# Softmax left unnormalised until after the value product, and the low part of q laid out on all 128 rows

## The chip, the cores and the metric

The kernel runs on one core of one Trainium2 chip. The metric is the time of one execution on the device in microseconds; three runs give a median. One further execution was taken by the hardware profiler, and every row below is from it.

## The reference

One decoder layer for 1024 tokens of width 1024, all in float32. The change lies in the attention, of which this is the part that matters (8 heads of 64):

```python
h = x @ w_in[i]                              # columns [q | k | v | u | z]
q = _partial_rope(q, positions); k = _partial_rope(k, positions)
scores = einsum(q, k) * (1.0 / math.sqrt(dh))        # three dilations, (window, dilation):
scores = where(mask, scores, NEG_INF)                # (128, 1), (512, 4), (2048, 16), causal
e = jnp.exp(scores - m)
den = jnp.sum(e, axis=-1, keepdims=True)
out = einsum(e / den, vb); lse = m + jnp.log(den)
attn = sum over dilations of softmax(lse) * out      # merged by the log-sum-exp weights
mix = jnp.concatenate([attn, gm], axis=-1) @ w_o[i]  # gm: a gated MLP beside the attention
x = _layernorm(ALPHA * x + mix, ln1_g[i], ln1_b[i])
```

Behind it come a gated feed-forward layer with a causal convolution over 2816 columns, a gate with a per-layer embedding, and two more layer norms.

## The kernel before

**Numbers in two parts.** TensorE multiplies in a reduced float32 (F32R). Each operand is therefore split into a high part, a rounded copy, and a low part, the rest. A full product is three matmuls into one PSUM bank (mm3, lines 132 to 134): high by high, high by low, low by high.

**Attention.** The merged dilations are one softmax over 1024 keys with an additive mask (0, log 2 or log 3 where one, two or three dilations see a key). Queries go in four row blocks I of 256 tokens (two parts of 128), and a unit is one row block and one head: 32 units, in order of I, then of head. Head h sits in pair p = h // 2; its 64 dimensions are partitions 0 to 63 for even heads and 64 to 127 for odd ones.

- K is kept as KE and KO. For even heads KE has K's high part in rows 0 to 63 and its low part in rows 64 to 127; KO is the mirror image for odd heads.
- q_post (line 452) transposes a block of q and writes QE and QO, which hold q's high part twice, and QL, which holds the low part of an even head in rows 0 to 63 and of the odd head of the same pair in rows 64 to 127. It is called from a list of slots (posts, line 881). Its ACT copies are issued at once, its DVE operations (rest) one slot later.
- unit_S (line 661) makes scores in chunks of up to 512 keys: L688 multiplies q's high part twice by K's high and low part (128 rows), L689 multiplies q's low part by K's high part alone (64 rows). DVE adds the mask, negates and takes the running minimum (L698).
- unit_exp (line 702) takes the exponential on ACT with the row sum in `den`, and unit_norm (line 707), one slot after it, takes the reciprocal (a power on POOL, L710) and multiplies both parts of the probabilities by it on POOL (L712).
- unit_T (line 714) transposes four 128 x 128 blocks of the probabilities on TensorE (L719); ACT and DVE split them.
- unit_PV (line 545) multiplies by V (L557). V's high and low part lie side by side, so rows 0 to 63 and 64 to 127 of the bank O each hold one part of the output, and unit_out (line 560) adds the two: ACT copies one half to `ot`, DVE adds (L570) into the mixture's page.

**What sets the order.** The schedule is manual: every engine runs its instructions in program order, and semaphores are added for the data. `attention` (line 743) goes through slots. In a slot it issues the scores of a unit up to three ahead, the DVE operations put off from the slot before (`later`), the exponentials and normalisations that are due, one unit_T, the unit_PV of three slots before, then a number of steps (pump) of a queue that fills TensorE: first the projections of q (q_dense, whose rotary embedding, rope, runs six operations on POOL), then, from unit 17 on, the output projections of finished row blocks (wo_up). `sides` advance beside it: the layer norm of finished blocks and the splits of the output weights on POOL (L537). The last row block's projection, wo_up(3), follows attention.

**Buffers.** Most tiles of attention are pages of 4 KB per partition, 24 in all under one tag: the parts of x not yet used, V's second half, q, the scores, the split probabilities. The banks S and O have two buffers each, and the transposes use three.

Of the kernel before, what the change touches and what calls it, by code (L numbers as in the profile page):

```python
# [51 lines left out]
def hybrid_layer(ctx, tc, x, xT, pT, pos, w_in, ln_z_g, ln_z_b, w_sT, b_sT, w_o,  # L52
# [98 lines left out]
    POOL.memset(neghalf, -0.5)  # L151
    negone = consts.tile([128, 2], F32, name="negone")
    POOL.memset(negone, -1.0)
# [295 lines left out]

    QE, QO, QL = {}, {}, {}  # L450

    def q_post(j, t):
        tok = q_toks[j]
        if t == 0:
            QE[j] = page([128, 4, 256], F32R, "qe")
            QO[j] = page([128, 4, 256], F32R, "qo")
            QL[j] = page([128, 4, 256], F32R, "ql")
        qe, qo, ql = QE[j], QO[j], QL[j]
        kt = tok_T(tok, t, "T")
        ts = slice(t * 128, (t + 1) * 128)  # L460
        copy(ACT, qe[0:64, :, ts], kt[0:64])
        copy(ACT, qo[64:128, :, ts], kt[64:128])
        copy(ACT, qo[0:64, :, ts], kt[64:128])

        def rest():
            copy(DVE, qe[64:128, :, ts], kt[0:64])
            DVE.tensor_tensor(ql[0:64, :, ts], kt[0:64], qe[0:64, :, ts].bitcast(F32), OP.subtract)
            DVE.tensor_tensor(ql[64:128, :, ts], kt[64:128], qo[64:128, :, ts].bitcast(F32), OP.subtract)
        return rest
# [70 lines left out]

    unit_state = {}

    mixes = {}

    def unit_PV(I, h, m, pt):
        st = unit_state[I, h]
        if m == 0:
            st["o"] = ps1("O")
        o = st["o"]
        for kb in (2 * m, 2 * m + 1):  # L550
            full = kb <= 2 * I
# [4 lines left out]
            for hl in range(2):  # L556
                PE.matmul(osl, v, pt[:, hl, src:src + wd], start=kb == 0 and hl == 0,  # L557
                          stop=kb == 2 * I + 1 and hl == 1)

    def unit_out(I, h):  # L560
# [5 lines left out]
        r, r2 = (slice(64, 128), slice(0, 64)) if odd else (slice(0, 64), slice(64, 128))  # L566
        ot = small.tile([128, 256], F32, name="ot", bufs=1)
        copy(ACT, ot[r], o[r2, 0:256])
        mix = mixes[I][r, p, :]
        later.append(lambda: DVE.tensor_tensor(mix, o[r, 0:256], ot[r], OP.add))  # L570

# [89 lines left out]
    def unit_S(I, h, chunk):  # L661
# [6 lines left out]
        K = KO if odd else KE  # L668
        r = slice(64, 128) if odd else slice(0, 64)
        q_lo = QL[I][r, p, ts]  # L670
        if part == 0 and c0 == 0:
            st["den"] = small.tile([128, 2], F32, name="den", bufs=5)
            st["nmx"] = small.tile([128, 4], F32, name="nmx", bufs=5)
# [14 lines left out]
        PE.matmul(o, q_hi, K[:, p, c0:c0 + w_], start=True, stop=False)  # L688
        PE.matmul(o, q_lo, K[r, p, c0:c0 + w_], start=False, stop=True)  # L689
        m0 = S - n + c0  # L690
# [11 lines left out]
    def unit_exp(I, h, part):  # L702
        st = unit_state[I, h]
        ACT.activation(st[part], st[part], AF.Exp, bias=st["m", part], scale=-1.0,
                       accum_out=st["den"][:, part:part + 1])

    def unit_norm(I, h):
        st = unit_state[I, h]
        rd = small.tile([128, 2], F32, name="rd", bufs=4)
        POOL.tensor_tensor(rd, st["den"], negone, OP.pow)  # L710
        for part in range(2):
            POOL.tensor_scalar(st[part], st[part], rd[:, part:part + 1], 1.0, op0=OP.mult, op1=OP.mult)  # L712

# [15 lines left out]
    due = []  # L729
# [13 lines left out]
    def attention(plan):  # L743
# [12 lines left out]
        for n in range(-3, len(units)):  # L756
# [8 lines left out]
            for m in range(banks):  # L765
# [8 lines left out]
                for v, ch in news[:take]:  # L774
                    if ch[3]:
                        due.append((slot + 1, "e", lambda v=v, p=ch[0]: unit_exp(*units[v], p)))
                        if ch[0] == 1:
                            due.append((slot + 2, "n", lambda v=v: unit_norm(*units[v])))
                news = news[take:]
# [633 lines left out]
```

## Time and profile before

| | |
|---|---|
| median of 3 runs | 1254.71 us (1254.49 to 1255.15) |
| the profiled execution | 1254.94 us |
| its span, first to last instruction | 1253.2 us |
| TensorE matmul busy | 1229.5 us, 98% |
| VectorE (DVE) busy | 795.9 us, 64% |
| ScalarE (ACT) busy | 539.4 us, 43% |
| GpSimd (POOL) busy | 546.3 us, 44% |
| mean granted clock of TensorE | 0.995 |

PE is TensorE's matmuls, PEld its weight loads. Times in the rows are us from the span's start unless marked ns. Matmuls overlap in the pipeline: the time of one runs from its start to its modelled end, so what a matmul costs in a stream is the distance to the next start. A bracket at the end of a timeline row is the time that the engine was idle before it and what released it; "issue" means that nothing the profile shows did. An entry x4 in a timeline merges four instructions.

### The profile page before, as it was taken

What the parts mean: (1) busy time and instruction counts of PE and PEld (TensorE: products, weight loads), DVE (VectorE), ACT (ScalarE), POOL (GpSimd) and SP (SyncE); (2) the same over time, 40 slices, a digit from 0 to 9 for tenths busy, and PEclk for the clock granted to TensorE, in tenths of its full rate; (3) what the DMA queues carried; (4) which work ended last, traced back from release to release, by engine and by line L of the source; (5) the groups of instructions that cost most, each with busy time, mean ns of one, the idle gap of its engine ahead of it and who ended that gap; (6) DMA issues with size and microseconds to landing.
All of it is one profiled execution on the core that took longest, in us unless ns stands there. A gap on an engine that the chain in (4) does not pass through costs nothing.

```text
span 1253.2 us, 15740 instructions
## 1 busy us (share of the span) xinstructions
PE 1229.5 (98%) x5804; PEld 1001.2 (80%) x5804; DVE 795.9 (64%) x1194; ACT 539.4 (43%) x921; POOL 546.3 (44%) x467
## 2 busy tenths in 40 slices
PE   9999999999999997999999999999999999999997
PEld 6888788877777777888888888888878888888886
DVE  4544422346877789566565566555667985797776
ACT  5322122367855663544434444444444354541221
POOL 2510000255727769576677776677610000022444
PEclk9999999999999998999999999999999999999998
DMA  7215511200200221221333321333479544640001
GB/s 272 68 51 183 185 35 35 68 18 1 85 35 17 85 101 68 69 85 55 114 126 126 127 64 63 126 127 126 133 261 313 205 129 126 228 159 17 35 34 51
DMA packets 61005, 131.70 MB, mean 105 GB/s; under 512 B 5376, under 2 KB 23168, under 8 KB 60928
## 3 DMA queue, kind: packets, MB, share of 16 engines
q1 hardware_dynamic: 58480, 122.17, 28.3%
q10 hardware_dynamic: 2448, 8.52, 2.0%
q8 instruction: 46, 0.75, 0.2%
q14 instruction: 31, 0.25, 0.1%
HBM read 97.90 MB, written 32.77 MB: 104 GB/s over the span
## 4 chain that ended last, share of the span: by engine, by line
PE 59%; DVE 2%; POOL 1%; issue 0%; ACT 0%; POOLq 0%; ACTq 0%
PE P L133 9%; PE P L134 9%; PE P L132 9%; PE D L134 7%; PE D L132 7%; PE D L133 7%; PE B L134 3%; PE B L132 3%; PE B L133 3%; PE B L860 1%; PE x2p L1266 0%; DVE th L1294 0%; DVE xop L868 0%; DVE wraw L951 0%; POOL rs L585 0%
## 5 line engine op out<-in xcount | busy, mean ns | idle before, releaser
L132 PE MATMUL P<-xop,wop 128*128 128x512 f32 (+1 forms) x360 | 138.9, 386 | 0.0
L134 PE MATMUL P<-xop,wop 128*128 128x512 f32 (+1 forms) x360 | 138.4, 384 | 0.0
L133 PE MATMUL P<-xop,wop 128*128 128x512 f32 (+1 forms) x360 | 138.4, 384 | 0.0
L168 POOL TENSOR_SCALAR rs<-mv 128x1 f32<-128x1 f32 x24 | 12.7, 529 | 265.3 <-DVE mv L166 265.3
L117 POOL TENSOR_TENSOR wop<-raw,wop 128x512 fp32r<-128x512 f32 x64 | 100.6, 1583 | 43.8 <-ACT wop L111 43.7
L117 POOL TENSOR_TENSOR wop<-s,wop 128x512 fp32r<-128x512 f32 x44 | 68.7, 1572 | 72.5 <-ACT wop L111 72.5
L111 ACT ACTIVATE aop<-raw 128x512 fp32r<-128x512 f32 x77 | 48.2, 626 | 91.7 <-DMA raw<-hid_d 56.8
L429 POOL TENSOR_TENSOR rt<-tok,cos_t 128x128 f32<-128x128 f32 x8 | 4.7, 589 | 177.8 <-ACT tok L488 166.7
L132 PEld LDWEIGHTS P<-xop,wop 128*128 128x128 f32 x360 | 67.6, 188 | 13.5 <-ACT ct L111 0.2
L134 PEld LDWEIGHTS P<-xop,wop 128*128 128x128 f32 x360 | 67.6, 188 | 13.4
L133 PEld LDWEIGHTS P<-xop,wop 128*128 128x128 f32 x360 | 67.6, 188 | 13.3
L132 PE MATMUL D<-xop,wop 128*128 128x512 f32 (+1 forms) x192 | 74.7, 389 | 0.0
L134 PE MATMUL D<-xop,wop 128*128 128x512 f32 (+1 forms) x192 | 73.8, 385 | 0.0
L133 PE MATMUL D<-xop,wop 128*128 128x512 f32 (+1 forms) x192 | 73.8, 384 | 0.0
L1014 POOL TENSOR_TENSOR ht<-ht,ct 128x1024 f32<-128x1024 f32 x22 | 65.9, 2994 | 15.2 <-ACT ht L1011 15.2
L133 PE MATMUL P<-bop,aop 128*128 128x512 f32 x176 | 68.7, 390 | 0.6 <-DVE bop L117 0.6
L117 DVE TENSOR_TENSOR aop<-raw,aop 128x512 fp32r<-128x512 f32 x77 | 54.5, 707 | 22.6 <-ACT aop L111 22.6
L132 PE MATMUL P<-bop,aop 128*128 128x512 f32 x176 | 68.6, 390 | 0.0
L134 PE MATMUL P<-bop,aop 128*128 128x512 f32 x176 | 68.5, 389 | 0.0
L111 ACT ACTIVATE wop<-raw 128x512 fp32r<-128x512 f32 x66 | 40.1, 631 | 63.0 <-DMA raw<-in_w_b_dram 35.5
L117 POOL TENSOR_TENSOR wop<-wraw,wop 128x512 fp32r<-128x512 f32 x44 | 57.0, 1303 | 7.4 <-ACT wop L111 5.1
L698 DVE CUSTOM_DVE_ANT_0 sp<-S,mask 128x512 f32<-128x512 f32 (+2 forms) x64 | 37.0, 588 | 35.7 <-PE S L689 31.7
(316 smaller groups left out, 3528.4 us busy)
## 6 DMA issues: line engine op xcount, KB each, us to landing
raw<-hid_d SPq DMA_DIRECT2D x35, 512.0 KB, 3.8
hid_d<-ct SPq DMA_DIRECT2D x22, 512.0 KB, 5.8
wd<-in_w_down_dram SPq DMA_DIRECT2D x44, 256.0 KB, 5.7
raw<-in_w_in_dram SPq DMA_DIRECT2D x18, 512.0 KB, 3.9
hid_d<-ht SPq DMA_DIRECT2D x33, 256.0 KB, 4.8
raw<-in_w_a_dram SPq DMA_DIRECT2D x11, 512.0 KB, 4.1
raw<-in_w_b_dram SPq DMA_DIRECT2D x11, 512.0 KB, 6.2
wraw<-in_w_a_dram SPq DMA_DIRECT2D x11, 512.0 KB, 6.0
```

Of the source, the lines that this page charges most:

```text
L111: ACT.activation(dst, src, AF.Copy)
L117: lo_eng.tensor_tensor(lo, src, hi.bitcast(F32), OP.subtract)
L132: PE.matmul(ps, sh, mh, start=first, stop=False, skip_group_check=chain)
L133: PE.matmul(ps, sh, ml, start=False, stop=False, skip_group_check=chain)
L134: PE.matmul(ps, sl, mh, start=False, stop=last, skip_group_check=chain)
L168: POOL.tensor_scalar(rs, mv[:, 1:2], eps, None, op0=OP.add)
L429: POOL.tensor_tensor(r[:, 0], x1, cb, OP.mult)
L698: DVE.tensor_tensor_reduce(dst, o, mask[:, m0:m0 + w_], op0=OP.add, op1=OP.min, accum_out=acc, scale=-1.0, scalar=prev)
L860: PE.transpose(ps[:, k * 128:(k + 1) * 128], src[:, k * 128:(k + 1) * 128], ident)
L1014: POOL.tensor_tensor(tt[g, e], tt[g, e], ctile[g, 1, e], OP.mult)
```

## The change

Three things are done. unit_norm goes: the probabilities stay as the exponential leaves them. The sums of both heads of a pair now stand in one tile, POOL takes the four reciprocals at once when the odd head's exponential is issued, and after the even head's last value product POOL spreads them to 64 columns for each head (`rb`); before the odd head's first value product TensorE transposes these two 128 x 128 blocks into the unused half of the odd head's bank O. unit_out then copies one half of the output into the mixture's page on ACT, adds the other on DVE, and for odd heads multiplies the pair's page by the transposed reciprocals on DVE. Last, QL becomes QLE and QLO, in which the low part of each head stands in both halves of the partitions (POOL copies it), so that L689 works on 128 rows and adds the product of the two low parts.

```diff
-    negone = consts.tile([128, 2], F32, name="negone")
+    negone = consts.tile([128, 4], F32, name="negone")
...
-            QL[j] = page([128, 4, 256], F32R, "ql")
+            QLE[j] = page([128, 4, 256], F32R, "qle")
+            QLO[j] = page([128, 4, 256], F32R, "qlo")
...
         def rest():
             copy(DVE, qe[64:128, :, ts], kt[0:64])
-            DVE.tensor_tensor(ql[0:64, :, ts], kt[0:64], qe[0:64, :, ts].bitcast(F32), OP.subtract)
-            DVE.tensor_tensor(ql[64:128, :, ts], kt[64:128], qo[64:128, :, ts].bitcast(F32), OP.subtract)
+            DVE.tensor_tensor(qle[0:64, :, ts], kt[0:64], qe[0:64, :, ts].bitcast(F32), OP.subtract)
+            DVE.tensor_tensor(qlo[64:128, :, ts], kt[64:128], qo[64:128, :, ts].bitcast(F32), OP.subtract)
+            copy(POOL, qle[64:128, :, ts], qle[0:64, :, ts].bitcast(F32))
+            copy(POOL, qlo[0:64, :, ts], qlo[64:128, :, ts].bitcast(F32))
...
         o = st["o"]
+        if m == 0 and h % 2:
+            rb = rbs.pop((I, h // 2))
+            for part in range(2):
+                PE.transpose(o[:, 256 + part * 128:384 + part * 128], rb[:, part, :], ident)
         for kb in (2 * m, 2 * m + 1):
...
+        if m == I and h % 2 == 0:
+            rb = rbs[I, h // 2] = small.tile([128, 2, 128], F32, name="rb", bufs=1)
+            copy(POOL, rb.rearrange("p a (b c) -> p a b c", c=64),
+                 rds.pop((I, h // 2))[:, :, :, None].to_broadcast([128, 2, 2, 64]))
...
-        ot = small.tile([128, 256], F32, name="ot", bufs=1)
-        copy(ACT, ot[r], o[r2, 0:256])
         mix = mixes[I][r, p, :]
-        later.append(lambda: DVE.tensor_tensor(mix, o[r, 0:256], ot[r], OP.add))
+        copy(ACT, mix, o[r2, 0:256])
+        later.append(lambda: DVE.tensor_tensor(mix, o[r, 0:256], mix, OP.add))
+        if odd:
+            both = mixes[I][:, p, :]
+            later.append(lambda: DVE.tensor_tensor(both, both, o[:, 256:512], OP.mult))
...
-        r = slice(64, 128) if odd else slice(0, 64)
-        q_lo = QL[I][r, p, ts]
+        q_lo = (QLO if odd else QLE)[I][:, p, ts]
...
-            st["den"] = small.tile([128, 2], F32, name="den", bufs=5)
+            if not odd:
+                dens[I, p] = small.tile([128, 2, 2], F32, name="den", bufs=4)
+            st["den"] = dens[I, p]
...
-        PE.matmul(o, q_lo, K[r, p, c0:c0 + w_], start=False, stop=True)
+        PE.matmul(o, q_lo, K[:, p, c0:c0 + w_], start=False, stop=True)
...
-                       accum_out=st["den"][:, part:part + 1])
-
-    def unit_norm(I, h):
-        st = unit_state[I, h]
-        rd = small.tile([128, 2], F32, name="rd", bufs=4)
-        POOL.tensor_tensor(rd, st["den"], negone, OP.pow)
-        for part in range(2):
-            POOL.tensor_scalar(st[part], st[part], rd[:, part:part + 1], 1.0, op0=OP.mult, op1=OP.mult)
+                       accum_out=st["den"][:, part, h % 2:h % 2 + 1])
+        if part == 1 and h % 2:
+            rd = rds[I, h // 2] = small.tile([128, 2, 2], F32, name="rd", bufs=5)
+            POOL.tensor_tensor(rd.rearrange("p a b -> p (a b)"),
+                               dens.pop((I, h // 2)).rearrange("p a b -> p (a b)"), negone, OP.pow)
...
-                        if ch[0] == 1:
-                            due.append((slot + 2, "n", lambda v=v: unit_norm(*units[v])))
```

## Rows read from the trace of the kernel before

**Rows 1.** The page, part 1: engine, busy us, share, instructions.
```profile
PE 1229.5 (98%) x5804; PEld 1001.2 (80%) x5804; DVE 795.9 (64%) x1194; ACT 539.4 (43%) x921; POOL 546.3 (44%) x467
```

**Rows 2.** Busy us (count) of PE, PEld, DVE, ACT, POOL; granted clock, DMA share, GB/s.
```profile
330.00:452.00 122.00, 121.75 (x665) 89.36 (x664) 93.83 (x225) 77.86 (x148) 72.24 (x81) 1.00 0.16 57
452.00:505.00 53.00, 44.14 (x290) 39.93 (x289) 49.23 (x63) 23.67 (x46) 48.33 (x38) 0.94 0.27 100
```

**Rows 3.** Timeline of TensorE late in attention: start us, duration us, line.
```profile
428.83 0.39 PE L134 MATMUL D<-wouh,mixl 128*128 128x512 f32 x1
429.06 0.40 PE L688 MATMUL S<-KO,qo 128*128 128x512 f32 x1
429.39 0.50 PE L689 MATMUL S<-KO,ql 64*128 64x512 f32 x1
429.82 0.66 PE L719 MATMUL B<-ident,sp 128*128 128x128 f32 x4
430.23 0.65 PE L557 MATMUL O<-pt,VP 128*128 128x256 f32 x4
```

**Rows 4.** Timeline of TensorE's weight loads, the same slot.
```profile
429.38 0.18 PEld L689 LDWEIGHTS S<-KO,ql 64*128 64x128 f32 x1 [0.36 <-issue]
```

**Rows 5.** Timeline of TensorE early in attention.
```profile
262.24 0.38 PE L689 MATMUL S<-KE,ql 64*128 64x256 f32 x1 [0.33 <-DVE ql L467]
...
264.02 0.22 PE L688 MATMUL S<-KO,qo 128*128 128x128 f32 x1
264.17 0.32 PE L689 MATMUL S<-KO,ql 64*128 64x128 f32 x1
264.42 0.39 PE L688 MATMUL S<-KO,qo 128*128 128x256 f32 x1
264.74 0.38 PE L689 MATMUL S<-KO,ql 64*128 64x256 f32 x1
265.05 0.50 PE L132 MATMUL O<-wih,xh 128*128 128x512 f32 x1
```

**Rows 6.** Tile S: duration ns min/median/max, first and last start, forms.
```profile
L689 PE MATMUL S<-KE,ql x48: 323/466/502, 261.1 to 441.2; 64*128 64x512 f32 x24, 64*128 64x128 f32 x8, 64*128 64x256 f32 x8, 64*128 64x384 f32 x8
```

**Rows 7.** Groups by form on POOL, 258 to 465 us: count, busy us, mean ns.
```profile
L537 POOL TENSOR_TENSOR woul<-raw,wouh 128x512 fp32r<-128x512 f32 x8 | 10.2, 1288 | 6.0 <-ACT wouh L111 5.9
...
L712 POOL TENSOR_SCALAR sp<-sp,rd 128x512 f32<-128x512 f32 x8 | 5.6, 698 | 0.0
...
L712 POOL TENSOR_SCALAR sp<-sp,rd 128x256 f32<-128x256 f32 x8 | 3.9, 483 | 0.0
```

**Rows 8.** Timeline of POOL, the power behind the rotary operations.
```profile
296.22 0.70 POOL L710 TENSOR_TENSOR rd<-den,negone 128x2 f32<-128x2 f32 x1
```

**Rows 9.** Timeline of DVE, the low part for the first scores.
```profile
261.50 0.68 DVE L467 TENSOR_TENSOR ql<-B,qe 64x512 fp32r<-64x512 f32 x1
```

**Rows 10.** Timeline of TensorE, the value product that follows rows 8.
```profile
297.47 0.65 PE L557 MATMUL O<-pt,VL 128*128 128x256 f32 x4
```

**Rows 11.** Groups on DVE, 258 to 452 us.
```profile
L570 DVE TENSOR_TENSOR mixf<-O,ot 64x256 f32<-64x256 f32 x28 | 11.7, 418 | 0.5
```

**Rows 12.** The view of rows 2 for L689 alone: PE and PEld only.
```profile
372.00:378.00 6.00, 1.96 (x5) 0.80 (x5) 1.00 0.47 175
408.00:414.00 6.00, 1.86 (x4) 0.67 (x4) 1.00 0.78 262
330.00:452.00 122.00, 26.45 (x58) 10.60 (x58) 1.00 0.16 57
```

**Rows 13.** The view of rows 2 in slices of 6 us.
```profile
342.00:348.00 6.00, 6.00 (x36) 4.54 (x36) 5.61 (x15) 5.40 (x12) 3.16 (x5) 1.00 0.02 8
...
372.00:378.00 6.00, 6.00 (x36) 4.50 (x37) 5.76 (x14) 4.98 (x11) 3.59 (x5) 1.00 0.47 175
408.00:414.00 6.00, 6.00 (x37) 4.41 (x37) 5.91 (x14) 5.97 (x11) 4.54 (x7) 1.00 0.78 262
```

**Rows 14.** Timeline of TensorE, the last output projection.
```profile
467.46 0.50 PE L134 MATMUL D<-wouh,mixl 128*128 128x512 f32 x1 [0.71 <-DVE mixl L637]
```

More of the change, by code (lines that the diff above doesn't have):

```diff
@@ L448, in k_post @@
         DVE.tensor_tensor(KO[0:64, :, ts], kt[64:128], KO[64:128, :, ts].bitcast(F32), OP.subtract)
-    QE, QO, QL = {}, {}, {}
+    QE, QO, QLE, QLO = {}, {}, {}, {}
     def q_post(j, t):
@@ L456, in q_post @@
             QO[j] = page([128, 4, 256], F32R, "qo")
-            QL[j] = page([128, 4, 256], F32R, "ql")
-        qe, qo, ql = QE[j], QO[j], QL[j]
+            QLE[j] = page([128, 4, 256], F32R, "qle")
+            QLO[j] = page([128, 4, 256], F32R, "qlo")
+        qe, qo, qle, qlo = QE[j], QO[j], QLE[j], QLO[j]
         kt = tok_T(tok, t, "T")
@@ L541, in hybrid_layer @@
     unit_state = {}
+    dens, rds, rbs = {}, {}, {}
     mixes = {}
```

## The prediction

> **What bounds the kernel now.** I read the page first. Its first part has TensorE busy for 98% of the span [rows 1], so what counts is whether a microsecond taken from TensorE's stream comes off the end, and whether another engine takes over where TensorE gets shorter. All edits lie in the attention stage, about 258 to 464 us, so the second view was the busy time of each engine in two stretches: the second part of attention, and the 53 us behind it [rows 2]. The reader is to see that TensorE is full in attention (121.75 of 122 us) at a granted clock of 1.00, which is 2.4 GHz, with DVE at 77% there; and that behind attention DVE (49.23 of 53) and POOL (48.33) carry the load while TensorE has holes. The second stage is tied to the end of attention by program order, so it should move earlier as a block.
>
> The third view is TensorE's timeline, read by starts: busy times overlap, but the distance from one start to the next is what a matmul costs. A product of 512 columns with all 128 rows comes 0.23 us before the next one (428.83 to 429.06) [rows 3]. The score products do not keep that pace. The low product uses only 64 rows: from L688 to L689 it is 0.33 us, from L689 to the transposes 0.43 us. A pair costs 0.76 us where two full-row products cost 0.46. The weight loads show the reason: the loader sits idle 0.36 us with no releaser and starts the 64-row load only when the matmul before it is through [rows 4]; elsewhere loads run ahead. The same holds for short chunks: two pairs of 128 and 256 columns take 1.03 us (264.02 to 265.05) [rows 5], where full-row products would by proportion take 0.12 and 0.06 us, so 0.36 us for the four (an estimate from the 0.23).
>
> **The change, part by part.**
>
> *Low part of q with all 128 rows.* Saved per pair: 0.30 us at 512 columns, 0.67/2 = 0.33 us at 128 and 256 [rows 3, 5]. The tile view counts 48 such products for even heads, half of them 512 wide, and its twin has 48 for odd heads [rows 6]. At 0.30 us, 96 pairs save 28.8 us. The bounds: if only the following matmul's delay went, 0.43 - 0.23 = 0.20 each, 19 us; at 0.33 each, 32 us. I take 28.8, since the full-row rows around it are the same shape as the new product.
>
> *A rule against this.* The Trainium skill, "TensorE: Matmul & The Clock Gate", section "Why this matters for your kernels", says that a single matmul with K=32 takes the same time as one with K=128, which would leave nothing to save by filling rows. By it the sum below would lose its 28.8 us, and the change would be a loss of 7 us (rival 4). This trace disagrees: a pair with a half-row product costs 0.30 us more from start to start [rows 3 to 5]. I go by the rows and keep the rule as a rival.
>
> *Transposed reciprocals.* Every pair of heads adds two 128-column transposes, in four blocks of four pairs: 32 in all. Four transposes take 0.41 us (429.82 to 430.23) [rows 3], so 32 add 3.3 us. They stand directly behind other transposes and before the value products, so no new switch of kind is added.
>
> *POOL.* It loses 64 multiplications over the probabilities (0.48 us at 256 columns, 0.70 at 512) and half of its 32 powers [rows 7, 8], and gains 16 powers over four columns, 16 broadcast copies of 256 columns and 16 copies of 512 columns from one half of the partitions to the other. The trace has no POOL copy across partitions: from below I take the one-input 0.70 us, from above the two-input 1.29 us [rows 7]; the copy has one input, so 0.70. POOL gets lighter in sum; it was not the bound, so that alone gives nothing. What counts is where TensorE now waits for POOL:
> - At the start the second block of q is the last thing TensorE waits for: L467 ends at 262.18, L689 follows at 262.24 after 0.33 us of idle [rows 5, 9]. The copy comes behind it and L689 waits 0.7 to 1.3 us more; what the pair saved before that point is lost in the wait too. The 1.29 us splits of the output weights stand behind these copies in POOL's queue; they wait longer, but serve output projections that come some 80 us later. With the second row block, needed one slot after its post, I put 2 us on q (1 to 4).
> - The broadcast copy of the reciprocals is issued one slot ahead of the odd head's first value product. Ahead of it in POOL's queue can be the six rotary operations: they end with a power starting at 296.22 [rows 8], it runs 0.70 us and rather more on four columns, then the copy of 0.48; that is 297.5 against a value product which stood at 297.47 [rows 10] and will stand about 0.8 us earlier. Two rotary blocks fall into attention's slots after the first: 1.5 us (0 to 4).
>
> The normalisation also goes from the chain between the exponential and the transposes. That wait is not seen on TensorE now, so it gives nothing by itself. Its power now stands one slot earlier in POOL's queue and waits there for the exponential as before.
>
> At nothing I put the larger constant, the reciprocals' layout and ACT's copy of half the output, which keeps its size and goes into the mixture's page instead of a buffer of its own; it is hidden by the slot that TensorE works ahead, and would cost its time once for each head if that lead were gone.
>
> *DVE and ACT.* The sum on DVE stays (0.418 us for 64 x 256) [rows 11] and the odd heads add 16 products of 128 x 256. DVE's cost goes by columns, so 0.42 each, 6.7 us in all (0.4 to 0.6 each for the bounds). On the average this is covered: in the second part 93.83 + 8 x 0.42 = 97 us against TensorE's 122 - 58 x 0.30 + 1.6 = 106 [rows 2, 12]. It is not covered everywhere. Where no projection products fill the slots, DVE is nearly full already: 5.61, 5.76 and 5.91 of 6 us in three slices, with ACT at 5.97 in the last [rows 13]. The last two have five and four pairs [rows 12], the first about as many, so TensorE would need only some 4.7 us there, and a slice can't shrink below what DVE and ACT need, 5.8 to 6.1. These three slices give back 3.4 us of the saving, and I add 1.6 for milder ones between them: 5 us together. Bounds: 2, if DVE makes it up in its idle time a slot later (the buffers allow one to two slots), and 9, if half of the DVE idle time that TensorE causes now stays. One more page per row block from the same 24 works in the same direction and is in this bound.
>
> *Behind attention.* The last odd head's product is one more 0.42 us in the chain to the last output projection, where TensorE already waits 0.71 us for DVE [rows 14]: 0.5 us (0 to 1.5). The rest of that stage moves as it is; its mean granted clock of 0.94 [rows 2] shows that a part of it runs at 1.2 GHz, in a stage whose TensorE has holes, and how much work meets that part may change by 2 us either way.
>
> **The sum** on the profiled execution's own time, 1254.94 us (span 1253.2, 1.7 us around it; 0.2 us above the median of 1254.71): -28.8 + 3.3 + 5 + 2 + 1.5 + 0.5 = -16.5. That gives 1238.4, or 1238 against the median.
>
> **The rivals.**
> 1. *Another engine becomes the bound throughout.* For it: the full slices of DVE and ACT [rows 13]. Against: 97 us of DVE in 106. If order on DVE keeps the nine lost microseconds and the q and reciprocal waits come at their upper ends: -28.8 + 3.3 + 9 + 4 + 4 + 1.5 = -7, about 1248. Chance 0.17.
> 2. *The gain comes whole.* DVE catches up, POOL's lighter load keeps its copies early: -28.8 + 3.3 + 2 + 1 = -22.5; with 0.33 us per pair -25: 1229 to 1232. For it: TensorE's waits are nearly nil now. Chance 0.13 for below 1231.
> 3. *Slower: POOL's in-order queue holds the reciprocals.* Place: the first value product of each of the 16 odd heads, behind which all of TensorE stands. Price: if two 128 x 512 POOL operations such as L537's, 2.6 us [rows 7], get in ahead, 16 x 2.6 = 42 us against the 22.5 of a whole gain: 1274. It decides from 1.4 us per odd head. For it: POOL is 59% busy in the second part [rows 2] and has the layer norm's operations there. Against: it loses work in sum, and the copy has a slot's lead of about 2.4 us. Chance 0.06.
> 4. *The rows don't matter.* The half-row product is slow for a reason that stays (its place among the transposes, its operands): no 28.8, and without a shorter TensorE no 5 of DVE, so 3.3 + 2 + 1.5 + 0.5 = 7 us more: 1262. Against: L688, full-row and in the same place, is only as slow as its successor's late load makes it [rows 3, 4]. Chance 0.04. The rule of the Trainium skill named above is this rival's ground.
>
> **How the numbers follow.** The likeliest, 1238 (its own range 1232 to 1244), has 0.60. What a measurement of this kernel can tell from no change is about 0.2%, 2.5 us. Rivals 3 and 4 are slower, 0.10, less 0.01 for mild forms that land near zero; with the worst of rival 1 that makes 0.03 for no change. Faster is 0.88, slower 0.09. The range, 1230 to 1249, leaves out rivals 3 and 4 (0.10), about half of rival 2 (0.06) and the end of rival 1 (0.03).
>
> **What would show each step.** In the changed profile L688 to L689 and L689 to its successor should both be 0.23 us at 512 columns, with the weight load ahead; a distance still at 0.33 or 0.43 refutes the main step. Attention should end near 447 us instead of 464, TensorE's new waits should name POOL's copy of q near 262 us and the copy of the reciprocals at some odd heads, and DVE should be the releaser of short TensorE holes in the slots without projection products. Wrong would make it: holes of over a microsecond before most odd heads' value products (rival 3), a granted clock of 0.5 in attention, or a copy across partitions on POOL that costs several microseconds.

## The result, and the profile after

The changed kernel takes 1242.18 us in the median (1241.51 to 1244.3, four runs) against 1254.93 us for the kernel before beside it (four runs): ratio 0.99, 95% interval 0.9882 to 0.9917, so 12.8 us or 1.0% faster. The forecast was 1238 in a range of 1230 to 1249. The profiled execution took 1241.51 us, 13.4 below the 1254.94 of the profiled one before; the forecast for that difference was 16.5. One of the seven runs of e2_norm_only below took 3137 us and is left out of its numbers.

The page's first part, answering to [rows 1]: TensorE is 23 us lighter, POOL has 48 instructions less.

```profile
PE 1206.2 (97%) x5836; PEld 1005.7 (81%) x5836; DVE 799.1 (64%) x1210; ACT 539.1 (43%) x921; POOL 508.8 (41%) x419
```

The windows answering to [rows 2], at the places where the same work now stands: early attention, its larger part, and the stage behind it.

```profile
258.00:320.00 62.00, 57.15 (x338) 48.73 (x337) 42.33 (x116) 45.17 (x118) 26.76 (x45) 1.00 0.03 10
320.00:449.00 129.00, 120.58 (x792) 105.39 (x791) 110.00 (x266) 91.68 (x176) 55.42 (x68) 1.00 0.18 61
449.00:491.00 42.00, 34.10 (x207) 30.11 (x207) 38.57 (x46) 13.85 (x28) 40.58 (x30) 0.92 0.28 104
```

TensorE, which was full in [rows 2], now has 8.4 us of idle time in 129 and DVE has come from 77% to 85%. The clock stays at 1.00 (2.4 GHz) in attention. Behind it the stage has moved as a block: a given product there starts 13.5 us earlier from 481 us to the end.

TensorE's timeline at one slot with a 512 and a 128 column chunk, answering to [rows 3]:

```profile
328.55 0.40 PE L703 MATMUL S<-KE,qe 128*128 128x512 f32 x1
328.78 0.40 PE L704 MATMUL S<-KE,qle 128*128 128x512 f32 x1
329.02 0.22 PE L703 MATMUL S<-KE,qe 128*128 128x128 f32 x1
329.08 0.28 PE L704 MATMUL S<-KE,qle 128*128 128x128 f32 x1
329.19 0.30 PE L731 MATMUL D<-ident,sp 128*128 128x128 f32 x1
```

The 512 pair takes 0.47 us (328.55 to 329.02) where it took 0.76, and the 128 pair 0.17. The weight loads, answering to [rows 4], now run ahead: the load for the low product at 328.78 begins at 328.55.

```profile
328.55 0.19 PEld L704 LDWEIGHTS S<-KE,qle 128*128 128x128 f32 x1
```

TensorE's waits between 255 and 460 us by releaser: total, times, longest (the seven largest groups). In the kernel before, the same view up to 475 us, where its attention has ended too, has 1.3 us before the last transposes of probabilities (`D`, here L731) and 0.7 before the last output projection (L134), which stay about as they were, and 0.3, 0.3, 0.2 and 0.2 us besides. The other groups are new or have grown.

```profile
PE S L703 <- DVE nmx L713: 4.3, 6, 1.0
PE O L557 <- POOL rb L113: 3.4, 4, 2.5
PE S L704 <- POOL qle L113: 2.0, 2, 1.0
PE D L731 <- DVE pt L735: 1.0, 1, 1.0
PE D L134 <- DVE mixl L651: 0.8, 1, 0.8
PE B L439 <- DVE qlo L469: 0.8, 1, 0.8
PE B L439 <- POOL tok L434: 0.6, 1, 0.6
```

Where the time of attention went, summed from start to start over all TensorE instructions from the first score product to the first product behind the last value product (260.9 to 464.0 before, 260.5 to 450.3 after), each distance put to the instruction that it follows:

| us | before | after | difference |
|---|---|---|---|
| 192 score products | 64.4 | 41.7 | -22.7 |
| 320 value products | 44.6 | 49.1 | +4.5 |
| 288 transposes of probabilities | 29.6 | 32.3 | +2.7 |
| 32 transposes of reciprocals | - | 2.5 | +2.5 |
| projections, and other transposes | 64.5 | 64.3 | -0.1 |

That is -13.3 for attention. Attention also begins 0.4 us earlier, which is not the edits' doing: at 135 us, where both kernels do the same work, the changed one's profiled execution is already 0.4 us ahead. In the runs below such differences ahead of attention reach 1.5 us.

The new holes stand inside these sums. TensorE's instructions come in the same order in both kernels, but for the 32 inserted transposes, so each distance can be set against its partner. Four of the new holes follow a score product (4.6 us); without them the pairs themselves saved 27.3. In a hole's length below, the normal distance is taken off.

### The profile page after: what moved, and what is told of

It is laid out like the page before. It is cut to its first block, busy times and chain, and to the rows that moved or that the text cites. A ratio compares the mean times of both kernels' runs of the same rounds, so it can differ in the third digit from the quotient of the medians.

```text
span 1239.8 us, 15718 instructions
## 1 busy us (share of the span) xinstructions
PE 1206.2 (97%) x5836; PEld 1005.7 (81%) x5836; DVE 799.1 (64%) x1210; ACT 539.1 (43%) x921; POOL 508.8 (41%) x419
## 3 DMA queue, kind: packets, MB, share of 16 engines
q1 hardware_dynamic: 58480, 122.17, 28.8%
## 4 chain that ended last, share of the span: by engine, by line
PE 87%; DVE 6%; ACT 3%; POOL 2%; issue 2%; DMA 1%; SPq 0%; POOLq 0%; ACTq 0%; DVEq 0%
PE D L132 10%; PE P L133 10%; PE P L134 10%; PE P L132 10%; PE D L134 9%; PE D L133 9%; PE B L132 4%; PE B L134 4%; PE B L133 4%; PE O L565 1%; PE ups L132 1%; PE kps L134 1%; PE kps L132 1%; PE ups L133 1%; PE kps L133 1%
## 5 line engine op out<-in xcount | busy, mean ns | idle before, releaser
L132 PE MATMUL P<-xop,wop 128*128 128x512 f32 (+1 forms) x360 | 138.9, 386 | 0.0
L134 PE MATMUL P<-xop,wop 128*128 128x512 f32 (+1 forms) x360 | 138.4, 384 | 0.0
L132 PEld LDWEIGHTS P<-xop,wop 128*128 128x128 f32 x360 | 67.6, 188 | 13.6 <-ACT ct L111 0.2
L134 PEld LDWEIGHTS P<-xop,wop 128*128 128x128 f32 x360 | 67.6, 188 | 13.5
L132 PE MATMUL D<-xop,wop 128*128 128x512 f32 (+1 forms) x192 | 74.5, 388 | 0.0
L134 PE MATMUL D<-xop,wop 128*128 128x512 f32 (+1 forms) x192 | 73.7, 384 | 0.0
L132 PE MATMUL P<-bop,aop 128*128 128x512 f32 x176 | 68.6, 390 | 0.0
L134 PE MATMUL P<-bop,aop 128*128 128x512 f32 x176 | 68.5, 389 | 0.0
L111 ACT ACTIVATE ct<-P 128x512 f32<-128x512 f32 x66 | 39.0, 591 | 43.9 <-PE P L134 43.9
```

Of the source, the lines that this page charges most:

```text
L111: ACT.activation(dst, src, AF.Copy)
L132: PE.matmul(ps, sh, mh, start=first, stop=False, skip_group_check=chain)
L134: PE.matmul(ps, sl, mh, start=False, stop=last, skip_group_check=chain)
```

## The experiments

The question after this result was not whether the pairs got faster, but why 3 us less came than forecast, and which half of the change pays.

**e1_low_only: the doubled low part alone.** The normalisation on POOL stays as in the kernel before.

```diff
-            QL[j] = page([128, 4, 256], F32R, "ql")
+            QLE[j] = page([128, 4, 256], F32R, "qle")
+            QLO[j] = page([128, 4, 256], F32R, "qlo")
...
-        PE.matmul(o, q_lo, K[r, p, c0:c0 + w_], start=False, stop=True)
+        PE.matmul(o, q_lo, K[:, p, c0:c0 + w_], start=False, stop=True)
```

> The kernel before with the doubled low part of q alone; the probabilities are still normalised on POOL. Theory A (the gain is the score pair's, the moved normalisation only costs): L688 to L689 and L689 to its successor 0.23 us at 512 columns, score stream 27 us shorter, given back 2.5 us at q's copies and 3 to 4 us where DVE and ACT fill the slots; no transposes, no waits for the reciprocals: 1232 to 1237, faster than the changed kernel's 1242. Theory B (the score pair is only shorter because POOL no longer stands between the exponential and the transposes): with POOL loaded as before, TensorE waits for the normalised probabilities and the time is 1243 or more.

Measured: 1247.12 us against 1255.43, ratio 0.994 (0.9927 to 0.9952). The half that holds the whole saving gives 8.3 us, less than both halves together. Theory A missed by 10 us. Theory B had the time and the wait, but not the reason: the pair is as short here as in the changed kernel (0.47 us at 512 columns). POOL's timeline shows what happens (the bracket is idle time and its releaser):

```profile
277.09 0.60 POOL L113 CAST qle<-qle 64x512 fp32r<-64x512 f32 x1 [4.32 <-DVE qle L468]
277.75 0.61 POOL L113 CAST qlo<-qlo 64x512 fp32r<-64x512 f32 x1
278.45 0.70 POOL L712 TENSOR_TENSOR rd<-den,negone 128x2 f32<-128x2 f32 x1
279.24 0.82 POOL L714 TENSOR_SCALAR sp<-sp,rd 128x128 f32<-128x128 f32 x2
...
288.62 0.60 POOL L113 CAST qle<-qle 64x512 fp32r<-64x512 f32 x1 [6.96 <-DVE qle L468]
```

and TensorE's timeline what it costs:

```profile
279.67 0.89 PE L721 MATMUL D<-ident,sp 128*128 128x128 f32 x3 [3.55 <-POOL sp L714]
...
291.20 1.14 PE L721 MATMUL D<-ident,sp 128*128 128x128 f32 x3 [1.42 <-POOL sp L714]
```

The copies of q's low part are issued ahead of the slot's normalisations. POOL goes by its order: the copy waits 4.3 and 7.0 us for DVE, the normalisations stand behind it although their exponentials are done (the last of them on ACT at 274.8, the normalisation at 278.45), and TensorE waits for the normalised probabilities. (The Trainium skill, "Perfetto Trace Analysis", section "Tensor Engine Instruction (MATMUL, LD_WEIGHTS)", calls GpSimd a strict FIFO; these rows agree.) The granted clock falls too, as the windows show:

```profile
272.00:282.00 10.00, 6.33 (x36) 5.21 (x36) 3.23 (x9) 4.15 (x13) 4.99 (x10) 0.94 0.01 2
282.00:292.00 10.00, 7.28 (x31) 5.28 (x31) 6.64 (x20) 5.70 (x18) 3.14 (x6) 0.84 0.00 0
```

**e2_norm_only: the unnormalised probabilities alone.** The changed kernel with the 64-row low part of the kernel before.

> The changed kernel with the low part of q on 64 rows again. Theory A: 32 transposes of 0.11 us (3.5 us) and 1 to 4 us of waits for the reciprocals, nothing gained: 1257 to 1262, slower than the kernel before. Theory B (less POOL work and a shorter chain to the transposes are worth something by themselves): 1254 or less.

Measured: 1258.3 us in the median of six runs, ratio 1.0027 (1.0016 to 1.0038), so about 3 us slower, as the theory of 32 added transposes had it; in its trace attention is 3.3 us longer, and the 16 places of the transposes make 3.5 of it. No wait for the reciprocals appears, which theory A had at 1 to 4 us. The halves alone give -8.3 and +3, about -5; together they give -12.8. The missing 8 us are the waits of e1_low_only, which go when POOL no longer stands between the exponential and the transposes, or when its order is changed (e9_low_only_order, below).

**e3_rb_early: the reciprocals spread earlier.** The changed kernel, with the spread copy issued at the start of the first slot in which its buffer is free, ahead of the powers due there, not behind the even head's last value product.

```diff
-        if m == I and h % 2 == 0:
-            rb = rbs[I, h // 2] = small.tile([128, 2, 128], F32, name="rb", bufs=1)
-            copy(POOL, rb.rearrange("p a (b c) -> p a b c", c=64),
-                 rds.pop((I, h // 2))[:, :, :, None].to_broadcast([128, 2, 2, 64]))
...
+    def spread():
+        if rb_wait and not rbs:
+            I, p = rb_wait.pop(0)
+            rb = rbs[I, p] = small.tile([128, 2, 128], F32, name="rb", bufs=1)
+            copy(POOL, rb.rearrange("p a (b c) -> p a b c", c=64),
+                 rds.pop((I, p))[:, :, :, None].to_broadcast([128, 2, 2, 64]))
...
+                spread()
                 for d in [d for d in due if d[0] <= slot]:
```

> The changed kernel with the copy that spreads the reciprocals issued at the start of the slot after the pair before has used its buffer, ahead of the power of that slot, not behind the even head's last value product. Theory A: TensorE's waits at the first value product of odd heads (0.4 + 0.7 + 2.7 + 0.4 us in the changed kernel's timeline) go to under 0.5 us in sum, and the time falls by 2.5 to 4 us to 1238 to 1240. Rival: these waits only stand in for DVE's, which come up right behind them; the holes go and others grow, 1241 to 1243.

Measured: 1239.16 us, ratio 0.9872 (0.9857 to 0.9887): about 3 us better than the changed kernel, with intervals that just touch. In the profiled executions attention is 2.0 us shorter (187.8 us against 189.8). The waits for `rb` are gone; one new hole of 1.4 us stands where the largest had been. In the changed kernel that largest one is seen in the two timelines, TensorE's and POOL's:

```profile
360.45 0.44 PE L557 MATMUL O<-ident,rb 128*128 128x128 f32 x2 [2.50 <-POOL rb L113]
```

```profile
358.59 0.61 POOL L113 CAST qle<-qle 64x512 fp32r<-64x512 f32 x1 [8.40 <-DVE qle L468]
359.32 0.61 POOL L113 CAST qlo<-qlo 64x512 fp32r<-64x512 f32 x1
360.00 0.40 POOL L113 COPY rb<-rd 128x256 f32<-128x256 f32 x1
360.36 1.00 POOL L723 TENSOR_TENSOR rd<-den,negone 128x4 f32<-128x4 f32 x1
```

It is the mechanism of e1_low_only again: q's copies at the head of POOL's queue wait 8.4 us for DVE, and the reciprocals stand behind them.

**e4_low_twice: what a half-row product costs.** The kernel before with its 64-row product issued twice, which adds the low part twice to the scores.

```diff
+        PE.matmul(o, q_lo, K[r, p, c0:c0 + w_], start=False, stop=False)
         PE.matmul(o, q_lo, K[r, p, c0:c0 + w_], start=False, stop=True)
```

> The kernel before with each 64-row low product issued twice in succession (its product is added twice, so the scores are other numbers). Theory A (the cost lies in going from 128 rows to 64 and back): the second 64-row product starts about 0.23 us after the first at 512 columns, the distances 0.33 before and 0.43 behind the pair stay, and the scores get 96 x 0.2 = 20 us longer or a little less. Rival (a half-row product is slow in itself): the second one costs 0.33 to 0.43 us too, 32 to 41 us longer. A third (a half-row product costs no more than a full one and something else makes the rows of before): no distance over 0.23 between the two and 0.33 and 0.43 not to be seen around them.

Measured: 1271.88 us in one run, its span 17.0 us above that of the kernel before. TensorE's timeline:

```profile
443.85 0.40 PE L688 MATMUL S<-KO,qo 128*128 128x512 f32 x1
444.17 0.49 PE L689 MATMUL S<-KO,ql 64*128 64x512 f32 x1
444.51 0.39 PE L690 MATMUL S<-KO,ql 64*128 64x512 f32 x1
444.83 0.44 PE L720 MATMUL B<-ident,sp 128*128 128x128 f32 x2
```

The three take 0.98 us (443.85 to 444.83), so a second 64-row product in a row adds 0.22 to the 0.76 of the pair: the price of a full-row product. The extra 0.30 us is paid once, for going from 128 rows to 64 and back. How it is spread over the distances (0.32, 0.34, 0.32) was not foreseen. The weight loads show both changes of rows: the load for the first 64-row product and that for the transposes behind come late, while the second 64-row load runs ahead.

```profile
444.17 0.18 PEld L689 LDWEIGHTS S<-KO,ql 64*128 64x128 f32 x1 [0.36 <-issue]
444.28 0.19 PEld L690 LDWEIGHTS S<-KO,ql 64*128 64x128 f32 x1
444.83 0.42 PEld L720 LDWEIGHTS B<-ident,sp 128*128 128x128 f32 x4 [0.36 <-issue]
```

The Trainium skill, "TensorEngine Tiling (Array Packing)", section "Key Properties", says that changing the tiling mode drains TensorE; these rows agree, if the 64-row product counts as such a change, and put 0.30 us on it.

**e5_fill: more products meant for the crowded slots.** e3_rb_early with what is done at unit 12 done at unit 14: the rest of the queue of q's projections is drained, and the loads and splits of the output weights begin. It was to leave TensorE other work in the slots where DVE is full.

```diff
-    attention({12: at_12, 17: at_17, 20: at_20, 25: at_25,
+    attention({14: at_12, 17: at_17, 20: at_20, 25: at_25,
```

> As e3_rb_early, and the rest of the projection of the last row block of q (drained at once at unit 12, with the loads of the output weights started there) is left in the queue until unit 14, so that it fills TensorE in some of the slots of units 12 and 13. Theory (the holes of 1 to 1.3 us at the score banks near 320 to 340 us come from DVE and ACT being full in slots without projection products): with filler in these slots part of the holes goes and the time falls by 1 to 3 us, to 1236 to 1238. Rival (the same work of DVE and ACT meets the same sum of TensorE's, only in another order; or the later loads of the output weights make new waits): within 1 us of e3_rb_early, or slower.

Measured: 1239.52 us, ratio 0.9873 (0.9861 to 0.9886): no gain, but the theory was not tested. The queue is already empty at unit 12: q's last projection starts at 313.3 us in both traces, and TensorE's 5836 matmuls come in the same order. Only the loads and splits moved (six of POOL's splits, L540, begin at 328.3 us where they began at 320.8). The holes between 324 and 339 us are 1.0, 1.0 and 1.7, where e3_rb_early has 1.0, 1.3 and 1.0.

**e6_low_only_dve: the second copy made by DVE.** e1_low_only with both halves subtracted by DVE, POOL's copies gone.

```diff
-            copy(POOL, qle[64:128, :, ts], qle[0:64, :, ts].bitcast(F32))
-            copy(POOL, qlo[0:64, :, ts], qlo[64:128, :, ts].bitcast(F32))
+            DVE.tensor_tensor(qle[64:128, :, ts], kt[0:64], qe[64:128, :, ts].bitcast(F32), OP.subtract)
+            DVE.tensor_tensor(qlo[0:64, :, ts], kt[64:128], qo[0:64, :, ts].bitcast(F32), OP.subtract)
```

> As e1_low_only, but the second copies of the low part are subtracted by DVE out of the transposes' bank, so that POOL does none of them. Theory C (in e1_low_only the normalisation stood in POOL's queue behind copies that waited 4 to 7 us for DVE): TensorE's waits for the normalised probabilities near 270 to 292 us (0.7 + 3.6 + 1.4 us and what follows them) go, DVE gets 11 us more, and the time falls from 1247 to 1240 to 1243. Rival (POOL's sum of work is too large for the shorter stage wherever the copies are made): no such fall, 1245 to 1249.

Measured: 1254.67 us, ratio 0.9998 (0.999 to 1.0007). The wait for POOL fell as expected, from 5.6 us (255 to 325) to 0.2, but the time missed the expectation by far: the longer chain on DVE made holes of its own, such as 2.3 us before L439 at 283.4 (`B`, released by DVE's `qlo`) and 3.1 at 372, and the mean granted clock between 258 and 325 us fell to 0.90. So the test of the queue by way of DVE failed; e9_low_only_order makes it without loading DVE.

**e7_no_mult: without DVE's 16 products.** e3_rb_early without the multiplication by the reciprocals, so that the attention output stays unnormalised.

```diff
-        if odd:
-            both = mixes[I][:, p, :]
-            later.append(lambda: DVE.tensor_tensor(both, both, o[:, 256:512], OP.mult))
```

> As e3_rb_early without the product of the pair's output and the transposed reciprocals on DVE (so the attention's output stays unnormalised, and all behind it works on other numbers). Theory (DVE is the bound in the slots without projection products and at the tail): 16 x 0.42 = 6.7 us less of DVE, of which about a third lies in such slots: 1 to 3 us less than e3_rb_early. Rival (DVE's share hardly matters, TensorE's order sets the time): within 0.5 us of it.

Measured: 1237.66 us, ratio 0.9857 (0.9843 to 0.9871), 1.5 us below e3_rb_early with overlapping intervals, so the two are not told apart. In the profiled executions attention is 1.8 us shorter, but the whole is not (1239.44 us against 1238.95). TensorE's wait for `nmx` goes only from 4.6 to 3.7 us: the added products are a small part of what fills DVE.

**e8_rb_early_dve: e3_rb_early with the second copy made by DVE.** The same edit as in e6_low_only_dve.

> As e3_rb_early, with the second copies of the low part subtracted by DVE as in e6_low_only_dve, none on POOL. Theory: TensorE's two waits for POOL's copy (1.27 and 1.22 us beyond the next start) shrink by 0.5 us each at most, since DVE needs 0.69 us for each of two more operations at the same place, and 11 us more on DVE cost about as much where DVE is full: within 1.5 us of e3_rb_early. Rival: the copies on POOL hold up more than these two waits, and the time falls by over 2 us.

Measured: 1253.3 us, ratio 0.9991 (0.998 to 1.0003): 14 us worse than e3_rb_early, which neither theory had. TensorE's timeline and windows at the start of attention:

```profile
262.57 0.38 PE L707 MATMUL S<-KE,qe 128*128 128x256 f32 x1 [1.11 <-DVE qe L113]
264.71 0.39 PE L708 MATMUL S<-KE,qle 128*128 128x256 f32 x1 [1.75 <-DVE qle L470]
...
265.24 0.63 PE L133 MATMUL O<-wil,xh 128*128 128x512 f32 x1
265.67 0.63 PE L134 MATMUL O<-wih,xl 128*128 128x512 f32 x1
```

```profile
262.00:264.00 2.00, 0.38 (x1) 0.19 (x1) 1.92 (x4) 0.82 (x1) 1.57 (x2) 1.00 0.00 0
264.00:268.00 4.00, 3.29 (x10) 2.70 (x11) 1.99 (x6) 0.99 (x4) 0.00 (x0) 0.64 0.38 131
```

After 2 us with one product the clock falls, and a 512-column product takes 0.43 us (265.24 to 265.67) in place of 0.23. The same happens from 293 to 297 us (0.65). In e3_rb_early all these windows read 1.00. So q's chain is dear on DVE twice: by its waits, and by the clock behind them. Between the two profiled executions 8 of the 13 us arise before 300 us; later holes, such as 2.8 us before L132 at 372, make the rest.

**e9_low_only_order: e1_low_only with another order on POOL.** Nothing is changed but the place of the copies: behind the normalisations due in the slot, not ahead of them.

```diff
-            copy(POOL, qle[64:128, :, ts], qle[0:64, :, ts].bitcast(F32))
-            copy(POOL, qlo[0:64, :, ts], qlo[64:128, :, ts].bitcast(F32))
+            twice.append(lambda: copy(POOL, qle[64:128, :, ts], qle[0:64, :, ts].bitcast(F32)))
+            twice.append(lambda: copy(POOL, qlo[0:64, :, ts], qlo[64:128, :, ts].bitcast(F32)))
...
                 for d in [d for d in due if d[0] <= slot]:
                     due.remove(d)
                     d[2]()
+                run_twice()
```

> The kernel before with the doubled low part alone (the normalisation stays on GpSimd, as in e1_low_only, 1247.1 us), but the copies of q's low part are issued on GpSimd behind the normalisations that are due in the same slot, not ahead of them. Theory C (in e1_low_only the copies waited for VectorE at the head of GpSimd's queue, and the normalisations behind them came late): TensorE's waits for GpSimd's sp between 258 and 325 us (6.7 us in six of them) fall below 2 us, the granted clock there is 0.99 or more, and the time is 1239 to 1244 us. Rival (GpSimd has too much to do with both jobs, whatever the order): the waits move to the copies or to later slots, and the time is 1245 to 1250 us.

Measured: 1238.76 us, ratio 0.9865 (0.985 to 0.988), 17.1 us below the kernel before and just below what theory C gave. (The 6.7 us of the expectation are those of the view up to 460 us; up to 325 us there were 5.6, in three waits.) POOL's timeline at the place of e1_low_only's first wait, and the windows:

```profile
272.96 0.70 POOL L719 TENSOR_TENSOR rd<-den,negone 128x2 f32<-128x2 f32 x1
273.76 0.83 POOL L721 TENSOR_SCALAR sp<-sp,rd 128x128 f32<-128x128 f32 x2
277.31 0.61 POOL L113 CAST qle<-qle 64x512 fp32r<-64x512 f32 x1 [2.72 <-DVE qle L475]
```

```profile
272.00:282.00 10.00, 9.14 (x59) 8.05 (x57) 5.40 (x18) 6.48 (x18) 6.65 (x14) 1.00 0.01 2
282.00:292.00 10.00, 8.72 (x49) 7.10 (x48) 7.59 (x21) 7.58 (x22) 7.03 (x13) 1.00 0.00 0
```

One more normalisation now runs ahead of the copy, TensorE's waits for `sp` between 258 and 325 us are 0.7 us where they were 5.6, and the clock stays at 1.00. POOL does all of its old work and the copies, and there is room for both.

**e10_rb_early_order: e3_rb_early with that order.**

> The version e3_rb_early (1239.2 us) with the copies of q's low part issued behind the reciprocals that are due in the same slot. Theory (nothing waits for those reciprocals in time there, their spread copies being early already): within 1 us of e3_rb_early, 1238 to 1240 us. Rival (the copies come later now, and the first score pair of a head waits for them): 1241 us or more, with a wait of TensorE for qle in the trace.

Measured: 1239.95 us, ratio 0.9873 (0.9858 to 0.9887): as e3_rb_early, as expected. Beside e9_low_only_order on the same chip it shows no gain from the deferred normalisation once POOL's order is right (1239.95 against 1238.76, intervals overlapping).

**e11_rb_early_order_post: the second half of row block 1 of q posted one unit earlier.** The edit moves that half's transposes, copies and subtractions ahead; the expectation describes the move the other way round.

```diff
-    posts = [(4, 1, 0), (6, 1, 1), (12, 2, 0), (15, 2, 1), (34, 3, 0), (37, 3, 1)]
+    posts = [(4, 1, 0), (5, 1, 1), (12, 2, 0), (15, 2, 1), (34, 3, 0), (37, 3, 1)]
```

> As e10_rb_early_order, with the transposes that follow the two first q chunks posted one unit later, so that TensorE has other work while VectorE and GpSimd finish q. Theory (the hole of 1.22 us near 284 us and that of 1.27 us near 262 us are q's chain alone): one or both go, and the time is 0.5 to 1.5 us below e10_rb_early_order, 1237 to 1239 us. Rival (the work put later meets the next chunk's transposes, and the wait is only moved): within 0.5 us of e10_rb_early_order or above it.

Measured: 1242 us, ratio 0.989 (0.9873 to 0.9906). The hole near 284 us is gone, but three others come before it in TensorE's timeline, and the clock falls behind them (windows):

```profile
275.44 0.63 PE L439 MATMUL D<-ident,tok 128*128 128x128 f32 x4 [1.30 <-DVE pt L747]
278.67 0.52 PE L743 MATMUL B<-ident,sp 128*128 128x128 f32 x3 [0.76 <-DVE qlo L476]
280.79 0.50 PE L132 MATMUL D<-wih,xh 128*128 128x512 f32 x1 [1.20 <-ACT tok L515]
```

```profile
282.00:285.50 3.50, 3.50 (x17) 3.23 (x16) 2.29 (x8) 1.67 (x6) 2.29 (x4) 0.58 0.00 0
```

The rival held: the wait was moved, and at a worse place.

## Why the prediction was right, and where its sizes were off

- **The score pairs, -28.8.** Right in place, and a little small. The pairs saved 27.3 us (0.47 us for 0.76 at 512 columns, 96 pairs). Another 3.7 us came from a place that the text did not count: where transposes follow a low product (70 times), the first of them took 0.165 us to the next one and now takes 0.11 (0.165 in e2_norm_only too, 0.11 in e1_low_only). Together -31.0. The cause was given as the half-row product whose weight load starts late; e4_low_twice sharpens it to the change between 128 and 64 rows and back. (The load in [rows 4] starts 0.08 us before the modelled end of the matmul ahead of it, so "through" says a little too much.) Rival 4, the rows that don't matter, is out.
- **The 32 transposes, +3.3.** 3.5 us in e2_norm_only and in e3_rb_early, where no wait stands among them. The 2.5 of the table is what follows them; the transpose of probabilities ahead of each two now takes 0.11 us to its successor, too, where it took 0.03.
- **Slices where DVE and ACT are full, +5.** Measured 5.4, in six holes before score products: 1.03, 1.20 and 1.04 us near 325, 331 and 339, then 0.55, 1.01 and 0.57 near 368, 374 and 401. Of this, 0.4 us stood before (L688 at 336.6, the hole at 331 now). The sum came out by two errors that cancel. The holes at 339, 368 and 401 lie in the three slices of [rows 13], moved forward, and make 2.2 us for the 3.4 of the forecast; the three outside those slices make 3.2 (2.8 over what stood before) where the text had 1.6 for milder ones. Three windows, in which DVE has 5.7 to 6.0 of 6 us and TensorE no longer fills its own:

```profile
330.00:336.00 6.00, 5.01 (x39) 4.53 (x38) 5.68 (x19) 5.13 (x12) 3.94 (x5) 1.00 0.75 258
368.00:374.00 6.00, 4.76 (x29) 3.83 (x29) 5.79 (x17) 4.90 (x11) 0.38 (x2) 1.00 0.31 127
401.00:407.00 6.00, 5.62 (x36) 4.71 (x37) 6.00 (x15) 5.52 (x10) 3.92 (x5) 1.00 0.53 169
```

  The step blamed the loss in part on the 16 new DVE products; e7_no_mult (3.7 us of the wait left) and e9_low_only_order (no such products, 3.9 us) show that the old work makes most of these waits. That DVE's fullness is their cause rests on the releaser in the trace: no run took them away.
- **q's copies, +2.** The two waits stood where the text put them (rows below), 1.27 and 1.22 us beyond the normal distance. Unforeseen were 0.7 and 1.0 us before L439, where q's next transposes wait for the rotary operations and for a bank that q's DVE operations still read: 4.2 in all, just over the upper bound of 4.

```profile
262.51 0.39 PE L704 MATMUL S<-KE,qle 128*128 128x256 f32 x1 [1.01 <-POOL qle L113]
...
284.49 0.50 PE L704 MATMUL S<-KE,qle 128*128 128x512 f32 x1 [0.96 <-POOL qle L113]
```

- **The reciprocals' copy, +1.5. This step was mis-sized, and its largest part was put in the wrong place.** It measured 4.1 us: 0.36, 0.65, 2.66 and 0.41 (4.4 with a slower first transpose behind each wait). The text queued the copy behind rotary operations, and there 0.65 us stand (at 318 us POOL's copy comes directly behind the sixth of them). The 2.66 us at 360 stand behind q's copies, which wait 8.4 us for DVE. Both were edits of the same change on the same queue, and they were costed one at a time. e3_rb_early takes this term out and gains 2 to 3 us.
- **The tail, +0.5.** The wait before the last output projection is 0.82 us where it was 0.71 [rows 14]; nothing else changed there, and the stretch at half clock behind attention stayed (mean granted clock 0.51 over 7 us in both).
- **Small holes of the kernel before** were counted at nothing. That before L132 at 280.5 us (0.4) is gone and that before the last transposes of probabilities is 0.3 shorter; those before L557 at 307.4 and L860 at 455.7 are still there, 0.2 and 0.1 longer.

Pairs -27.3, first transposes behind them -3.7, added transposes +3.5, full slices +4.9 (over what stood there before), q +4.2, reciprocals +4.4, the wait before L132 -0.4, everything else in attention +1.1: -13.3. With the -0.4 from ahead of attention and +0.2 behind it, that is the 13.4 of the profiled executions. So the forecast's nearness is luck in part: the terms of q's copies and of the reciprocals' came to 8.6 us where 3.5 were forecast, and 2.2 us more from the pairs covered nearly half of the difference. Rival 1 was half right: DVE became the bound in slices, not throughout. Rival 3 named the right queue, and its mechanism cost 4 us and not 42, since twelve of the 16 odd heads had their copy in time.

One step was right only by itself. Taking the normalisation out of the chain was put at nothing, because TensorE did not wait for it, and alone it gains nothing (e2_norm_only). But it kept q's copies from doing harm: with the normalisation at the same place in POOL's queue, the copies cost 8 us (e1_low_only). Order does the same: e9_low_only_order keeps the normalisation and gets more than the whole change did, 17.1 us against 12.8, with intervals that do not overlap. What stays open is the rest of q's chain, the two waits of 1.2 us; neither DVE (e6_low_only_dve, e8_rb_early_dve) nor an earlier post (e11_rb_early_order_post) removed them with a gain.

## What to carry to other kernels

On an engine that works in order, cost the edits of one change together: list what each one waits for and what is queued behind it, and issue an operation that waits for a slow producer behind the work that is ready. Where a product with fewer rows stands alone among full-row ones, fill its rows or put several such products together. When the fullest engine gets shorter, read the next one by slices, since a mean of 85% here hid slices at 95 to 100%.

## What the runs showed of the hardware that was not expected

- A product of 64 rows between products of 128 costs 0.30 us extra, a second one behind it only 0.22 in all (512 columns, e4_low_twice). Where transposes follow, the first of them is 0.055 us slower as well. The weight load runs ahead between two products of 64 rows, and is late at each change of rows.
- Short holes can cost the clock as well as themselves: e8_rb_early_dve (two waits of 1.1 and 1.75 us with one product between), e11_rb_early_order_post and e1_low_only each show the granted clock falling towards 0.5, the 1.2 GHz level, inside attention. The changed kernel's idle 2.50 us at 360 did not: its windows over attention read 1.00. Length alone does not tell: in e6_low_only_dve a hole of 2.34 us before 283.4 was followed by 0.50 over 3.4 us, while in e8_rb_early_dve 2.24 us at the same place, and 2.78 before 372, were followed by 1.00.
- POOL copies 64 x 512 from one half of the partitions to the other in 0.61 us, below the 0.70 taken as lower bound; its power over four columns takes 1.02 us where two columns took 0.70 [rows 8]. The groups by form on POOL (258 to 452 us):

```profile
L723 POOL TENSOR_TENSOR rd<-den,negone 128x4 f32<-128x4 f32 x16 | 16.3, 1016 | 32.9 <-ACT sp L719 32.7
...
L113 POOL CAST qle<-qle 64x512 fp32r<-64x512 f32 x8 | 4.9, 610 | 40.2 <-DVE qle L468 40.2
```
